# Turning 30 blocks by VectorE and transfers in place of TensorE transposes, in a two-layer decoder trunk

## The chip, the cores and the metric

The kernel runs on one core of a Trainium2 chip, as one program. The metric is the time of one execution in microseconds of the device. A core has TensorE (matrix products, and transposes as products with an identity), VectorE, ScalarE, GpSimd and SyncE, each with an instruction queue of its own that it works off in order, and 16 DMA engines for transfers. Transfers are issued here by SyncE (all weights), by GpSimd (rows and scratch) and a few by ScalarE.

## The reference

Two layers over 256 tokens of width 2048 and 256 memory tokens, in float32:

```python
h = x
for layer in range(2):
    u = rmsnorm(h, norm_mix[layer])
    mix = hgrn2_gdn_mixer(u, ...) if layer == 0 else mamba2_mixer(u, ...)
    h = h + mix
    h = h + memory_cross_attention(rmsnorm(h, norm_xattn[layer]), rmsnorm(mem, norm_mem[layer]),
                                   xa_wq[layer], xa_wk[layer], xa_wv[layer], xa_wo[layer])
    h = h + swiglu(rmsnorm(h, norm_ffn[layer]), ffn_w_gate[layer], ffn_w_up[layer], ffn_w_down[layer])
return rmsnorm(h, norm_final)

def swiglu(h, w_gate, w_up, w_down):              # 2048 -> 5632 -> 2048
    return (silu(h @ w_gate) * (h @ w_up)) @ w_down

def memory_cross_attention(h, m, wq, wk, wv, wo): # 4 heads of 128
    q, k, v = h @ wq, m @ wk, m @ wv
    p = softmax(q k^T / sqrt(128))                # per head
    return (p v) @ wo

def mamba2_mixer(u, ...):                         # 4096 inner, 8 groups of 512
    z, xbc, dt = split(u @ w_in)
    x, B, C = split(silu(conv(xbc) + bias))
    y = ssd_chunked(x, softplus(dt + dt_bias), -exp(a_log), B, C) + d_skip * x
    return rmsnorm(y * silu(z), norm_w) @ w_out
```

## The kernel before, in words

**Products.** TensorE does nearly everything. A float32 weight tile (128 x 1024 numbers, 512 KB, tile `wr`, four buffers) is loaded by SyncE's queue. `split` makes two tiles of a faster matmul type of it: `wh`, a cast by ScalarE (line 156), and `wl = wr - wh`, by VectorE (recorded at line 124); both have four buffers. Activations are kept as such a pair too, hi and lo, in `u` tiles (16 buffers of 4 x 256 numbers per partition). `xstat` (matmuls recorded at line 121) computes 256 tokens by 512 columns in two accumulators `acc`: for each 128 rows of the weights and each half of the tokens three matmuls, xh wh, xh wl and xl wh. A product over all 2048 rows is 16 x 2 x 3 = 96 matmuls, and one weight tile feeds 12.

**Turning.** `xstat` yields rows (tokens on partitions), but its own operand must have channels on partitions. So results are turned between products. `turned` (line 289) does it for one block, 2 x 128 tokens by 512 channels, with 8 `pe.transpose` of 128 x 128 into PSUM, in two calls of 4. Four kinds of block are turned:

- *Feed-forward activations.* `ffn` takes the 5632 hidden channels in 11 blocks, in groups of 4, 4 and 3. For each block: the gate product, SiLU by ScalarE into `sg` (tile `gate`, `raw` or `w`, in turn), the up product, and `sg = sg * up` by VectorE. `turn(sg)` is called one block later, between the gate and the up product of the next block, and for the last block of a group after its up product: `turned`, then `split` into a `u` pair (ScalarE copy, VectorE subtraction). Then the group is multiplied by its part of the down weights, added to `h` for four column blocks `nb`.
- *Residual blocks.* `RowNorm.block` turns a block of `h`, scales by the norm's gain (ScalarE writes hi, VectorE lo) and sums squares; it is called as each column block `nb` of a sub-layer's last projection is added to `h`. N3 feeds the second mixer, N4 the second cross-attention.
- *Gate blocks of the second mixer.* `ssd` works in 8 groups of 512 channels. `group` projects x, convolves it, builds decay matrices, computes y, and multiplies it by silu(z), where z comes through `columns`: `rows` evicts the product into the tile `raw` by ScalarE (line 403), `turned` turns `raw` into the PSUM tile `tn`, and VectorE multiplies. After four groups the first half of the output projection runs, after the other four the second half.
- *Queries and keys* of the two cross-attentions, through `columns` as well, copied by ScalarE into `cv` and `X`.

**Order.** The kernel is written in dataflow; a planner orders each engine's instructions by priority (program order) along a simulated timeline and inserts the waits. Engines then work in exactly that order. Tiles of one tag share its buffers, and a new tile waits until all readers of the one before are done.

Of the kernel before, what the change touches and what calls it, by code (L numbers as in the profile page):

```python
# [9 lines left out]
F32 = mybir.dt.float32  # L10
# [3 lines left out]
AF = mybir.ActivationFunctionType  # L14
ALU = mybir.AluOpType
# [3 lines left out]
P = 128  # L19
# [59 lines left out]
def trunk(ctx: ExitStack, tc: tile.TileContext, A: dict, out: bass.AP):  # L79
    nc = tc.nc  # L80
# [4 lines left out]
    up = ctx.enter_context(tc.tile_pool(name="u", bufs=16))  # L85
# [30 lines left out]
    def col(name, i=0, n=1):  # L116
        o = COLS[name][0] + i
        return cols[:, o:o + n]
# [4 lines left out]
    def tt(e, o, a, b, op):  # L123
        e.tensor_tensor(o, a, b, op=op)  # L124

    def stt(o, a, s, b, op0, op1):
        dve.scalar_tensor_tensor(o, a, s, b, op0=op0, op1=op1)  # L127

    def t4(tag, shape, dt=F32):
        return mp.tile(shape, dt, name=tag, tag=tag, bufs=BUFS.get(tag, 1))  # L130
# [24 lines left out]
    def split(hi, lo, src):  # L155
        act.copy(hi, src)  # L156
        tt(dve, lo, src, hi.bitcast(F32), ALU.subtract)
# [96 lines left out]
    class Norm:  # L254
# [9 lines left out]
        def block(self, nb):  # L264
            src = self.load(nb)
            hi, lo = utiles()
            for c in range(4):
                g = col(self.gain[0], self.gain[1] + nb * 4 + c)
                act.activation(hi[:, c], src[:, c], AF.Copy, scale=g)
                stt(lo[:, c], src[:, c], g, hi[:, c].bitcast(F32), ALU.mult, ALU.subtract)  # L270
            self.u.append((hi, lo))
# [10 lines left out]
    def turned(src, i, ps=None, late=0):  # L282

        if ps is None:
            ps = psb([P, 2, T])
        for x in range(2):
            c = 2 * i + x
            for a in range(2):
                ins = pe.transpose(ps[:, x, a * P:(a + 1) * P], src[a][:, c * P:(c + 1) * P], ident)  # L289
                if late:  # L290
                    later_in_stream(ins, late)
        return ps

    class RowNorm:


# [4 lines left out]
            self.ss = cp.tile([P, 2, 4], F32, name="rss", tag="rss", bufs=2)  # L301
            self.r = None

        def block(self, nb, src, late=0):
            op = utiles()
            hi, lo = op
            for i in range(2):
                ps = turned((src[:, 0], src[:, 1]), i, None, late)
                for x in range(2):
                    c = 2 * i + x  # L310
                    g = col(self.gain[0], self.gain[1] + nb * 4 + c)
                    act.activation(hi[:, c], ps[:, x], AF.Copy, scale=g)  # L312
                    stt(lo[:, c], ps[:, x], g, hi[:, c].bitcast(F32), ALU.mult, ALU.subtract)
            self.u.append(op)
            self.squares(nb, src)
# [91 lines left out]
    def rows(N, W, n0, func=AF.Copy, first=None):  # L407

        accs = xstat(W, n0, 512, N.u)
        if first:  # L410
            first()
        r = N.column()
        o = t4("raw", [P, 2, 512])
        o = [o[:, 0], o[:, 1]]
        evict(o, accs, r, func)
        return o

    def columns(N, W, n0, func=AF.Copy, first=None, late=0):

        o = rows(N, W, n0, func, first)  # L420
        for i in range(2):
            yield i, turned(o, i, pt.tile([P, 2, T], F32, name="tn", tag="tn"), late)

    def heads_by_token(N, W, n0, c0):

# [387 lines left out]
    def memory_keys(layer):  # L813

        def load_mem(nb):
            raw = wp.tile([P, 4, T], F32, name="wr", tag="wr", bufs=4)
            nc.sync.dma_start(raw, blk(A["memT"], nb))
            return raw

        M = Norm(("norm_mem", 16 * layer), load_mem, mem_r[0])  # L820
        k = t4("X", [P, 4, T])
        for i, ps in columns(M, ("xa_wk", layer), 0):
            act.copy(k[:, 2 * i:2 * i + 2], ps)
        return M, k

    def xattn(layer, N, nxt, keys=None):
        q = t4("cv", [P, 4, T])
        for i, ps in columns(N, ("xa_wq", layer), 0):
            act.copy(q[:, 2 * i:2 * i + 2], ps)
        M, k = keys or memory_keys(layer)  # L830
        pT = [t4(tg, [P, 4, T]) for tg in ("D", "MD")]
        pr = t4("kq", [P, 2, 4, T])
        sc = float(P) ** -0.5
        sm = cp.tile([P, 2, 4], F32, name="xsm", tag="xsm")
        mx = cp.tile([P, 2, 4], F32, name="xmx", tag="xmx")
        for a in range(2):
            for i in range(2):
                ps = psb([P, 2, T])
                for x in range(2):
                    m = 2 * i + x  # L840
                    mm(ps[:, x], q[:, m, a * P:(a + 1) * P], k[:, m])
                mi = mx[:, a, 2 * i:2 * i + 2]
                dve.tensor_reduce(mi, ps, axis=AX.X, op=ALU.max)
                dve.tensor_scalar(mi, mi, -sc, None, op0=ALU.mult)
                for x in range(2):
                    m = 2 * i + x
                    act.activation(pr[:, a, m], ps[:, x], AF.Exp, bias=mx[:, a, m:m + 1], scale=sc,
                                   accum_out=sm[:, a, m:m + 1])
        for a in range(2):
            dve.reciprocal(sm[:, a], sm[:, a])  # L850
            tt(dve, pr[:, a], pr[:, a], sm[:, a].unsqueeze(2).to_broadcast([P, 4, T]), ALU.mult)
            for b in range(2):
                ps = psb([P, 4, P])
                for m in range(4):
                    pe.transpose(ps[:, m], pr[:, a, m, b * P:(b + 1) * P], ident)
                (act.copy if b else dve.tensor_copy)(pT[b][:, :, a * P:(a + 1) * P], ps)
        v = gate_rows(M, ("xa_wv", layer), 0, AF.Copy, "XT")
        hi, lo = utiles()
        for i in range(2):
            ps = psb([P, 2, T])  # L860
            for x in range(2):
                m = 2 * i + x
                for b in range(2):
                    mm(ps[:, x], v[:, b, m * P:(m + 1) * P], pT[b][:, m], x == 0 and b == 0, b == 1)
            split(hi[:, 2 * i:2 * i + 2], lo[:, 2 * i:2 * i + 2], ps)
        project(("xa_wo", layer), [(hi, lo)], ((0, 4),), lambda nb: nxt.block(nb, h[nb]))


    def ffn(layer, N, done=None, parts=None, by_token=None):
        b0 = 0  # L870
        for nblk in (4, 4, 3):
            hid = []
            late = None

            def turn(sg):
                hi, lo = op = utiles()
                for i in range(2):
                    split(hi[:, 2 * i:2 * i + 2], lo[:, 2 * i:2 * i + 2], turned(sg, i))
                hid.append(op)

            for b in range(b0, b0 + nblk):
                ga = xstat(("ffn_w_gate", layer), 512 * b, 512, N.u)
                r = N.column()
                sg = t4(("gate", "raw", "w")[b % 3], [P, 2, 512])
                sg = (sg[:, 0], sg[:, 1])
                for a in range(2):
                    act.activation(sg[a], ga[a], AF.Silu, scale=r[:, a:a + 1])
                if late:
                    turn(late)
                ua = xstat(("ffn_w_up", layer), 512 * b, 512, N.u)  # L890
                for a in range(2):
                    stt(sg[a], ua[a], r[:, a:a + 1], sg[a], ALU.mult, ALU.mult)
                late = sg
            turn(late)
            last = b0 + nblk == 11
            project(("ffn_w_down", layer), hid, ((4 * b0, 4 * nblk),), done if last else None, parts if last else None)
            if last and by_token:
                project_by_token(("ffn_w_down", layer), hid, 4 * b0, 4 * nblk, parts, by_token)
            b0 += nblk


    def ssd(N, nxt):
# [30 lines left out]
        def group(g, bct):  # L933
# [22 lines left out]
            for half in range(2):  # L956
# [11 lines left out]
                for x in range(2):  # L968
                    m = 2 * half + x
                    stt(y[:, m], xc[:, m], col("ssd_d", 4 * g + m), ps[:, x], ALU.mult, ALU.add)  # L970
            for i, z in columns(N, W, 512 * g, AF.Silu):
                tt(dve, y[:, 2 * i:2 * i + 2], y[:, 2 * i:2 * i + 2], z, ALU.mult)
            hi, lo = utiles()
            for m in range(4):
                w = col("ssd_norm", 4 * g + m)
# [21 lines left out]
        for nb in range(4):  # L997
            accs = xstat(Wo, nb * 512, 512, ys, (KT, KT))
            for a in range(2):
                p, hb = part[nb][:, a], h[nb][:, a]  # L1000
                tt(dve, p, p, accs[a], ALU.add)
                stt(hb, p, r[:, a:a + 1], hb, ALU.mult, ALU.add)
            nxt.block(nb, h[nb])


    def load_x(nb):
# [24 lines left out]
    N2 = RowNorm(("norm_ffn", 0))  # L1031
    xattn(0, N1, N2, keys)
    N3 = RowNorm(("norm_mix", 16))
    ffn(0, N2, lambda nb: N3.block(nb, h[nb]))
    N4 = RowNorm(("norm_xattn", 16))
    ssd(N3, N4)
    N5 = RowNorm(("norm_ffn", 16))
# [83 lines left out]
```

## Time and profile before

| | |
|---|---|
| median of 3 runs | 2910.77 us (2910.56 to 2910.94) |
| profiled execution: time, span | 2911.57 us, 2909.8 us |
| TensorE busy, granted clock | 2891.2 us (99%), 0.998 |
| VectorE, ScalarE, GpSimd busy | 1770.2, 1457.6, 28.9 us |
| matmuls of `xstat` (line 121) | 7808 with wh and 3904 with wl |
| transposes of `turned` (line 289) | 608 |
| transferred | 542.36 MB, mean 186 GB/s |
| transfers issued by GpSimd | 14.69 MB, 1.6% of the 16 engines' span |

Engines: PE is TensorE's matmuls, PEld its weight loads, DVE VectorE, ACT ScalarE, POOL GpSimd, SP SyncE, and a q behind a name is the engine's queue. In a group "out<-in" names the tile written and the tiles read (`cst` holds the identity), then come partitions x elements, the count, busy us, mean ns of one, and the idle time before. Matmul records overlap, since matmuls are pipelined: what one costs is read from the starts, not from its length.

### The profile page before, as it was taken

The numbers are of one execution on the slowest core, as the hardware profiler recorded it, in microseconds if no ns is written. First come the engines' busy times: TensorE is split into PE (matmuls) and PEld (weight loads), VectorE is DVE, ScalarE is ACT, GpSimd is POOL, SyncE is SP. The second block draws the span as 40 slices with busy tenths as digits, with TensorE's granted clock in tenths as the row PEclk, the third lists the DMA queues.
The fourth block names the chain that finished last, engine by engine and source line by source line (L and its number), as shares of the span: only waits on it lengthen the run. The fifth ranks groups of instructions, "written<-read, shape, count | busy, mean of one in ns | idle before, by whom it ended". The sixth has DMA issues, their size and how long they took to land.

```text
span 2909.8 us, 35776 instructions
## 1 busy us (share of the span) xinstructions
PE 2891.2 (99%) x13656; PEld 2402.2 (83%) x13656; DVE 1770.2 (61%) x2287; ACT 1457.6 (50%) x1834; POOL 28.9 (1%) x61
## 2 busy tenths in 40 slices
PE   8999999999999999999999999999999999999998
PEld 7888888888888888888888888888888888888887
DVE  6676768865555445445677846787664454455455
ACT  7455547655443443444655645565564443443444
POOL 0000000000000000000000000000000000000000
PEclk9999999999999999999999999999999999999999
DMA  8554544545555555555655555545555555555554
GB/s 284 173 175 141 182 145 164 191 159 188 188 188 195 188 189 192 192 189 187 206 180 195 188 198 186 188 167 182 204 185 190 189 189 194 191 190 191 195 188 153
DMA packets 154749, 542.36 MB, mean 186 GB/s; under 512 B 16968, under 2 KB 23248, under 8 KB 154576
## 3 DMA queue, kind: packets, MB, share of 16 engines
q1 hardware_dynamic: 149872, 525.11, 52.2%
q0 software_dynamic: 4288, 14.69, 1.6%
q8 instruction: 107, 1.75, 0.2%
q14 instruction: 66, 0.54, 0.1%
q10 hardware_dynamic: 416, 0.27, 0.0%
HBM read 536.13 MB, written 3.87 MB: 186 GB/s over the span
## 4 chain that ended last, share of the span: by engine, by line
PE 98%; DVE 1%; ACT 1%; issue 0%; DMA 0%; SPq 0%; DVEq 0%
PE acc L121 91%; PE mx L121 4%; PE mx L289 1%; PE tn L289 1%; PE mx L952 0%; DMA wr<-in_hy_w_in 0%; DVE wl L124 0%; ACT wh L156 0%; DVE tmp L124 0%; PE mx L489 0%; DVE b L127 0%; PE mx L601 0%; DVE X L127 0%; DVE D L124 0%; ACT D L448 0%
## 5 line engine op out<-in xcount | busy, mean ns | idle before, releaser
L121 PE MATMUL acc<-wh,u 128*128 128x512 f32 x7808 | 2445.8, 393 | 7.2 <-ACT wh L156 7.2
L124 DVE TENSOR_TENSOR wl<-wr,wh 128x1024 fp32r<-128x1024 f32 x974 | 1191.3, 1224 | 979.3 <-ACT wh L156 975.9
L121 PEld LDWEIGHTS acc<-wh,u 128*128 128x128 f32 x7808 | 1465.0, 188 | 306.3 <-ACT wh L156 7.2
L156 ACT CAST wh<-wr 128x1024 fp32r<-128x1024 f32 x978 | 1025.6, 1050 | 1210.6 <-PE acc L121 1145.1
L121 PE MATMUL acc<-wl,u 128*128 128x512 f32 x3904 | 1530.8, 392 | 1.3 <-DVE wl L124 1.3
L121 PEld LDWEIGHTS acc<-wl,u 128*128 128x128 f32 x3904 | 735.2, 188 | 151.7 <-DVE wl L124 2.7
L127 DVE SCALAR_TENSOR_TENSOR cv<-tn,cols,cv 128x255 f32<-128x255 f32 (+2 forms) x120 | 57.6, 480 | 19.3 <-ACT cv L395 17.3
L124 DVE TENSOR_TENSOR h<-h,acc 128x512 f32<-128x512 f32 (+1 forms) x89 | 57.6, 675 | 10.5 <-PE acc L121 10.3
L403 ACT ACTIVATE raw<-acc,r 128x512 f32<-128x512 f32 x64 | 42.2, 684 | 23.7 <-PE tn L289 12.0
L127 DVE SCALAR_TENSOR_TENSOR u<-mx,cols,u 128x256 fp32r<-128x256 f32 x96 | 43.2, 479 | 10.4 <-ACT u L312 6.8
L312 ACT ACTIVATE u<-mx,cols 128x256 fp32r<-128x256 f32 x80 | 34.8, 469 | 20.5 <-PE mx L289 18.1
L289 PE MATMUL tn<-cst,raw 128*128 128x128 f32 x272 | 43.7, 272 | 1.0 <-ACT raw L403 1.0
L289 PEld LDWEIGHTS tn<-cst,raw 128*128 128x128 f32 x272 | 34.1, 139 | 10.2 <-ACT raw L403 1.4
L124 DVE TENSOR_TENSOR u<-mx,u 128x512 fp32r<-128x512 f32 x48 | 31.0, 684 | 12.2 <-ACT u L156 12.2
L156 ACT CAST u<-mx 128x512 fp32r<-128x512 f32 x48 | 26.0, 591 | 16.1 <-PE mx L289 10.7
L319 ACT ACTIVATE b<-h 128x512 f32<-128x512 f32 x48 | 29.9, 624 | 1.4 <-DVE h L127 1.4
L121 PEld LDWEIGHTS mx<-tmp 128*127 128x127 f32 (+7 forms) x240 | 24.8, 178 | 1.3 <-issue 0.7
L289 PE MATMUL mx<-cst,h 128*128 128x128 f32 x160 | 25.3, 272 | 0.0
L121 PE MATMUL mx<-tmp 128*127 128x64 f32 (+7 forms) x240 | 25.0, 260 | 0.0
L127 DVE SCALAR_TENSOR_TENSOR kq<-tn,cols,kq 128x255 f32<-128x255 f32 (+2 forms) x48 | 22.8, 475 | 2.4 <-ACT kq L395 2.0
L289 PEld LDWEIGHTS mx<-cst,h 128*128 128x128 f32 x160 | 20.0, 140 | 4.9
L395 ACT ACTIVATE cv<-tn,cols 128x256 f32<-128x256 f32 x40 | 18.6, 466 | 5.2 <-PE tn L289 3.9
(281 smaller groups left out, 1129.0 us busy)
## 6 DMA issues: line engine op xcount, KB each, us to landing
wr<-in_ffn_w_gate SPq DMA_DIRECT2D x176, 512.0 KB, 3.2
wr<-in_ffn_w_up SPq DMA_DIRECT2D x176, 512.0 KB, 3.2
wr<-in_ffn_w_down SPq DMA_DIRECT2D x176, 512.0 KB, 3.2
wr<-in_ssd_w_in SPq DMA_DIRECT2D x161, 512.0 KB, 3.3
wr<-in_hy_w_in SPq DMA_DIRECT2D x129, 512.0 KB, 3.3
wr<-in_ssd_w_out SPq DMA_DIRECT2D x64, 512.0 KB, 3.3
wr<-in_hy_w_out SPq DMA_DIRECT2D x32, 512.0 KB, 4.1
tmp<-rows POOLq DMA_DIRECT2D x18, 512.0 KB, 4.1
```

The costliest lines, as they stand in the source:

```text
L121: return pe.matmul(o, lhsT=lhsT, rhs=rhs, start=start, stop=stop, skip_group_check=True)
L124: e.tensor_tensor(o, a, b, op=op)
L127: dve.scalar_tensor_tensor(o, a, s, b, op0=op0, op1=op1)
L156: act.copy(hi, src)
L289: ins = pe.transpose(ps[:, x, a * P:(a + 1) * P], src[a][:, c * P:(c + 1) * P], ident)
L312: act.activation(hi[:, c], ps[:, x], AF.Copy, scale=g)
L319: act.activation(t4("b2", [P, 512]), src[:, a], AF.Square, accum_out=self.ss[:, a, nb:nb + 1])
L395: act.activation(c, x, AF.Copy, scale=w[:, 3:4])
L403: act.activation(o[a], accs[a], func, scale=r[:, a:a + 1])
```

## The change

A helper `turned_by_dma` turns a block without TensorE. VectorE transposes 32 x 32 blocks of both halves into y, four GpSimd-issued transfers write the four partition groups of y to a DRAM tile (1 KB runs), a fifth reads it back as z (4 KB per partition), and z has channels on partitions, in tokens by 32. y and z take the tiles named in `tags`, or two `u` buffers. `by32` is a view that matches the order. It is used for these blocks; all others stay on TensorE:

- feed-forward, both layers: every block but the last of each group, so 8 of 11 a layer;
- residual blocks: `nb` 0 to 2 of N3 and of N4, where the subtraction is also cut into halves of 128 tokens;
- gate blocks: three of each four groups, 6 of 8;
- the keys of layer 0 and the queries of layer 1.

```diff
+    def turned_by_dma(src, tags):
+        if tags:
+            y, z = t4(tags[0], [P, 1024]), t4(tags[1], [P, 1024])
+        else:
+            y, z = (up.tile([P, 1024], F32, name="ut", tag="u") for _ in range(2))
+        y, z = y.rearrange("p (b k a c) -> p b k a c", b=4, k=4, a=2), z.rearrange("p (q k c) -> p q k c", q=4, k=8)
+        for a in range(2):
+            dve.transpose(y[:, :, :, a, :].rearrange("p b k c -> p k b c"), src[a])
+        d = dp.tile([4, 32, 4, 256], F32, name="turns", tag="turns", bufs=2)
+        for q in range(4):
+            nc.gpsimd.dma_start(d[:, :, q].rearrange("b r x -> r b x"),
+                                y[32 * q:32 * q + 32].rearrange("r b k a c -> r b (k a c)"))
+        nc.gpsimd.dma_start(z.rearrange("p q k c -> p (q k c)"), d.rearrange("b r q x -> (b r) (q x)"))
+        return z.rearrange("p q k c -> p k q c")
+
+    AWAY = (("X", "cv"), ("tmp", "tmp"))
+
+    def by32(x):
+        return x.rearrange("p k (a q c) -> p (k a) q c", a=2, q=4)
...
-        def block(self, nb, src, late=0):
+        def block(self, nb, src, late=0, tags=None):
             op = utiles()
             hi, lo = op
-            for i in range(2):
+            if tags:
+                z = turned_by_dma((src[:, 0], src[:, 1]), tags)
+                for c in range(4):
+                    g, x = col(self.gain[0], self.gain[1] + nb * 4 + c), z[:, 2 * c:2 * c + 2]
+                    act.activation(by32(hi[:, c:c + 1]), x, AF.Copy, scale=g)
+                    for a in range(2):
+                        stt(by32(lo[:, c:c + 1])[:, a], x[:, a], g, by32(hi[:, c:c + 1])[:, a].bitcast(F32), ALU.mult, ALU.subtract)
+            for i in range(0 if tags else 2):
                 ps = turned((src[:, 0], src[:, 1]), i, None, late)
...
+    def columns_by_dma(N, W, n0, func=AF.Copy, tags=None):
+        z = turned_by_dma(rows(N, W, n0, func), tags)
+        for i in range(2):
+            yield i, z[:, 4 * i:4 * i + 4]
...
-        for i, ps in columns(M, ("xa_wk", layer), 0):
-            act.copy(k[:, 2 * i:2 * i + 2], ps)
+        if layer:
+            for i, ps in columns(M, ("xa_wk", layer), 0):
+                act.copy(k[:, 2 * i:2 * i + 2], ps)
+        else:
+            for i, z in columns_by_dma(M, ("xa_wk", layer), 0, tags=("tmp", "w")):
+                act.copy(by32(k[:, 2 * i:2 * i + 2]), z)
...
-            def turn(sg):
+            def turn(sg, b):
                 hi, lo = op = utiles()
-                for i in range(2):
-                    split(hi[:, 2 * i:2 * i + 2], lo[:, 2 * i:2 * i + 2], turned(sg, i))
+                if b < b0 + nblk - 1:
+                    z = turned_by_dma(sg, AWAY[b % 2])
+                    for i in range(2):
+                        split(*(by32(x[:, 2 * i:2 * i + 2]) for x in op), z[:, 4 * i:4 * i + 4])
+                else:
+                    for i in range(2):
+                        split(hi[:, 2 * i:2 * i + 2], lo[:, 2 * i:2 * i + 2], turned(sg, i))
                 hid.append(op)
...
-            for i, z in columns(N, W, 512 * g, AF.Silu):
-                tt(dve, y[:, 2 * i:2 * i + 2], y[:, 2 * i:2 * i + 2], z, ALU.mult)
+            away = g % 4 < 3
+            for i, z in (columns_by_dma if away else columns)(N, W, 512 * g, AF.Silu):
+                o = by32(y[:, 2 * i:2 * i + 2]) if away else y[:, 2 * i:2 * i + 2]
+                tt(dve, o, o, z, ALU.mult)
...
-            nxt.block(nb, h[nb])
+            nxt.block(nb, h[nb], 0, AWAY[nb % 2] if nb < 3 else None)
...
-    ffn(0, N2, lambda nb: N3.block(nb, h[nb]))
+    ffn(0, N2, lambda nb: N3.block(nb, h[nb], 0, AWAY[nb % 2] if nb < 3 else None))
```

The queries of `xattn` are changed like the keys, with the layers the other way round.

More of the change, by code (lines that the diff above doesn't have):

```diff
@@ L827, in xattn @@
         q = t4("cv", [P, 4, T])
-        for i, ps in columns(N, ("xa_wq", layer), 0):
-            act.copy(q[:, 2 * i:2 * i + 2], ps)
+        if layer:
+            for i, z in columns_by_dma(N, ("xa_wq", layer), 0, tags=("tmp", "w")):
+                act.copy(by32(q[:, 2 * i:2 * i + 2]), z)
+        else:
+            for i, ps in columns(N, ("xa_wq", layer), 0):
+                act.copy(q[:, 2 * i:2 * i + 2], ps)
         M, k = keys or memory_keys(layer)
@@ L873, in ffn @@
             late = None
-            def turn(sg):
+            def turn(sg, b):
                 hi, lo = op = utiles()
-                for i in range(2):
-                    split(hi[:, 2 * i:2 * i + 2], lo[:, 2 * i:2 * i + 2], turned(sg, i))
+                if b < b0 + nblk - 1:
+                    z = turned_by_dma(sg, AWAY[b % 2])
+                    for i in range(2):
+                        split(*(by32(x[:, 2 * i:2 * i + 2]) for x in op), z[:, 4 * i:4 * i + 4])
+                else:
+                    for i in range(2):
+                        split(hi[:, 2 * i:2 * i + 2], lo[:, 2 * i:2 * i + 2], turned(sg, i))
                 hid.append(op)
@@ L888, in ffn @@
                 if late:
-                    turn(late)
+                    turn(late, b - 1)
                 ua = xstat(("ffn_w_up", layer), 512 * b, 512, N.u)
@@ L893, in ffn @@
                 late = sg
-            turn(late)
+            turn(late, b)
             last = b0 + nblk == 11
```

## The prediction

> **What bounds the kernel now.** I read the page's first part, its chain, and then the waits of TensorE and of ScalarE. The first two lines below are the page's head and its first part, the third heads its chain. The others are waits: who waited for whom, total us, times, longest us.
>
> ```profile
> span 2909.8 us, 35776 instructions
> ...
> PE 2891.2 (99%) x13656; PEld 2402.2 (83%) x13656; DVE 1770.2 (61%) x2287; ACT 1457.6 (50%) x1834; POOL 28.9 (1%) x61
> ...
> PE 98%; DVE 1%; ACT 1%; issue 0%; DMA 0%; SPq 0%; DVEq 0%
> ```
> ```profile
> ACT wh L156 <- PE acc L121: 1145.1, 702, 5.0
> ...
> PE acc L121 <- ACT wh L156: 7.2, 1, 7.2
> PE acc L121 <- DVE wl L124: 1.3, 2, 0.9
> PE tn L289 <- ACT raw L403: 1.0, 1, 1.0
> ```
> TensorE is never out of work: 18.6 us of the span are not busy, and its longest wait, 7.2 us, happened once. The weight casts of ScalarE wait for TensorE instead, 702 times: each stands ready until a weight buffer comes free. So a matmul taken off TensorE shortens the kernel by the time it takes there, provided nobody else becomes late, and work added to VectorE, ScalarE, GpSimd or the transfers costs nothing until it makes TensorE wait.
>
> **What is removed.** One block (512 channels of 256 tokens) is turned by 8 transposes of 128x128. The lines view has them all, by target and source (busy us, mean ns); the chain in order of time shows what a block costs.
>
> ```profile
> L289 PE MATMUL tn<-cst,raw 128*128 128x128 f32 x272 | 43.7, 272 | 1.0 <-ACT raw L403 1.0
> ...
> L289 PE MATMUL mx<-cst,h 128*128 128x128 f32 x160 | 25.3, 272 | 0.0
> ...
> L289 PE MATMUL mx<-cst,raw 128*128 128x128 f32 x64 | 8.9, 272 | 0.0
> ...
> L289 PE MATMUL mx<-cst,gate 128*128 128x128 f32 x64 | 8.6, 272 | 0.0
> ...
> L289 PE MATMUL mx<-cst,w 128*128 128x128 f32 x48 | 6.2, 273 | 0.0
> ```
> ```profile
> 728.68 43.58 PE acc L121 x192
> 773.13 43.54 PE acc L121 x192
> ```
> ```profile
> 1346.50 0.22 PE mx L289 x2
> 1346.72 0.23 PE acc L121
> 1346.95 0.66 PE mx L289 x6
> ```
> ```profile
> 1566.53 0.44 PE tn L289 x4
> ```
> In the feed-forward blocks the first run of matmuls ends at 728.68 + 43.58 = 772.26 and the next begins at 773.13, so 8 transposes take 0.87 us. A residual block takes 0.22 + 0.66 = 0.88 us, and a block that goes through tile tn 2 x 0.44 = 0.88 us. That is 0.11 us each, though each record is 272 ns long: the records overlap.
>
> The count: a feed-forward layer has groups of 4, 4 and 3 blocks and keeps the last of each on TensorE, so 3 + 3 + 2 = 8 go per layer, 16 in two (128 of the 64 + 64 + 48 = 176 transposes). Three residual blocks go before the second mixer and three behind it (48 of 160); six gate blocks, one of keys and one of queries go from tile tn (64 of 272). Together 30 blocks, 240 transposes, 30 x 0.88 = 26.4 us, all on the path that sets the end.
>
> [...]
>
> **What takes its place, per block.** Two VectorE transposes of 128x512 (32x32 within themselves), four GpSimd-issued writes of 128 KB to DRAM, then, behind all four, one read of 512 KB, and then the same copies and subtractions as before, from SBUF rather than PSUM. The nearest rows, from the lines view and from the DMA part (KB, us from issue to landing):
>
> ```profile
> L658 DVE STREAM_TRANSPOSE XT<-X 128x512 f32<-128x512 f32 x4 | 2.8, 707 | 0.1
> ...
> L661 DVE STREAM_TRANSPOSE XT<-X 32x128 f32<-32x128 f32 x8 | 2.4, 303 | 0.2
> ```
> ```profile
> L635 POOL DMA_DIRECT2D X<-scratch x4 | 3.0, 761 | 5.4 <-PE acc L121 3.6 <-DMA scratch<-b 1.9
> ```
> ```profile
> q1 hardware_dynamic: 149872, 525.11, 52.2%
> ...
> scratch<-MD POOLq DMA_DIRECT2D x4, 256.0 KB, 3.1
> X<-scratch POOLq DMA_DIRECT2D x4, 256.0 KB, 5.6
> ```
> ```profile
> L127 DVE SCALAR_TENSOR_TENSOR u<-mx,cols,u 128x256 fp32r<-128x256 f32 x96 | 43.2, 479 | 10.4 <-ACT u L312 6.8
> ...
> L127 DVE SCALAR_TENSOR_TENSOR b<-mx,hms,gate 128x128 f32<-128x128 f32 x24 | 6.5, 344 | 0.1
> ```
> A transpose that writes in pieces costs between 0.71 us (the plain one) and 4 x 0.303 = 1.21 us (four of the small ones for 512 columns). I take 0.71, the same element count. VectorE gets 30 x 1.41 = 42 us, at most 73. In the six residual blocks 8 subtractions of 128 columns replace 4 of 256: 8 x 0.344 - 4 x 0.479 = 0.84 us each, 5 us together. ScalarE keeps its instructions. VectorE goes from 61% to about 62.5% of the span.
>
> GpSimd issues 150 more transfers, 150 x 0.76 = 114 us beside its 28.9: off the path. The read waits at the head of GpSimd's queue for the writes, and what is queued behind it are the next turn's writes and, in the mixer, the row loads of the next heads. The engines that carry the transfers are at 52% for the weight queue. The turns move 30 x 1 MB, 31.5 MB on 525 MB, so about 3 points more at the same rate. I put no price on that; against the weights it would have to hold up their loads, which are prefetched four deep.
>
> The length of one turn: 1.41 (transposes) + 4 x 0.76 (issues) + 3.1 (last write) + 5.6 (read) = 13.2 us; at most 14.2 with the slower transposes. Then come the consumers.
>
> **Where that is hidden.** For a turn to cost nothing, 13.2 us plus the consumers must fit between the source's last write and the first read of the result. Rows of the timeline (start us, us), in the order residual, gate, keys, queries:
>
> ```profile
> 1376.42 0.68 DVE L124 TENSOR_TENSOR h<-h,acc 128x512 f32<-128x512 f32 x1
> 1393.31 3.04 PE L121 MATMUL acc<-u,wh 128*128 128x256 f32 x24
> ```
> ```profile
> 1541.99 0.69 ACT L403 ACTIVATE raw<-acc,r 128x512 f32<-128x512 f32 x1
> 1561.64 0.68 DVE L124 TENSOR_TENSOR X<-X,tn 128x512 f32<-128x512 f32 x1
> ```
> ```profile
> 555.90 1.37 ACT L403 ACTIVATE raw<-acc,mem_r 128x512 f32<-128x512 f32 x2 [0.94 <-PE acc L121]
> 615.51 0.81 PE L121 MATMUL mx<-X,cv 128*128 128x256 f32 x3
> 2092.84 1.25 ACT L403 ACTIVATE raw<-acc,r 128x512 f32<-128x512 f32 x2
> 2125.73 1.03 PE L121 MATMUL mx<-X,cv 128*128 128x256 f32 x4
> ```
> Feed-forward: the turn of the last but one block of a group is handed over, at the latest, behind the last block's gate product. Its up product follows, half of the 192 matmuls above, 21.8 us, before the down projection starts, which reads that block as its second or third. 13.2 fits.
>
> Gates: 1542.7 to 1561.6 is 18.9 us, 5.7 to spare. Keys have 58 us, queries 31.
>
> Residual: the tight one is the third block before the second mixer. h is ready at 1377.1, and the small product at 1393.3 reads that block from its 17th matmul, about 1395.3: 18.2 us, for 13.2 plus about 2.5 of copies and subtractions (eight of 0.344 us). If VectorE is a weight subtraction late, or a landing slower, TensorE loses 0 to 3 us there, once. I take 1, as the margin of 2.5 is about as large as either. The other residual blocks have a whole block's matmuls more.
>
> **The sum.** 26.4 removed, 1 given back: 25.4. The profiled execution took 2911.57 us (span 2909.8 and 1.8 around it), 0.8 above the median of the runs. So 2886.2 for a profiled execution, 2885.4 against the median of 2910.77: forecast 2885.5. The bounds of this case alone: 0 to 5 us given back, and at most 2 us more gained where matmuls just behind transposes run slower; 2882 to 2890.
>
> **Rivals.**
> *A queue blocked by a late transfer (slower).* ScalarE and VectorE take instructions in a written order that an estimate of the transfers fixed. If a turn lands later than booked, the copy out of z stands at the head of ScalarE's queue (in the gates, the product on VectorE's), and the weight casts and subtractions behind it stop. The trace shows what such a stop costs:
>
> ```profile
> 322.53 1.23 DVE L124 TENSOR_TENSOR wl<-wr,wh 128x1024 fp32r<-128x1024 f32 x1 [1.50 <-ACT wh L156]
> 329.42 0.71 DVE L638 STREAM_TRANSPOSE XT<-X 128x512 f32<-128x512 f32 x1 [5.66 <-DMA X<-scratch]
> 330.05 1.18 DVE L124 TENSOR_TENSOR wl<-wr,wh 128x1024 fp32r<-128x1024 f32 x1
> ```
> VectorE stood 5.66 us for a transfer, its weight subtraction came 6.3 us after the previous one had ended, and TensorE has no wait there. So a cushion of about 6 us is proven. The rival needs a stop above 6 + 25.4/30 = 6.9 us on average in all 30 turns, half the turn's 13.2. With 8 us it is 30 x 2 = 60 lost, 34.6 net, 2945 us. For it: a turn has two transfers in a row, and neither their shape nor their booking is in this trace. Against it: the same round through DRAM cost 0.34 to 5.66 us of waiting here, the latter behind an issue that was itself 3.6 us late.
>
> *VectorE becomes the bound in the mixer.*
> ```profile
> 1550.00:1600.00 50.00, 50.00 (x254) 40.93 (x253) 39.96 (x54) 30.08 (x40) 1.06 (x2) 1.00 0.57 189
> ```
> In a steady stretch of groups (columns PE, PEld, DVE, ACT) VectorE is busy 39.96 of 50 us; 1.41 more is 41.4. It has room, but it works in bursts. If each of the six turned gates cost TensorE the transposes' time and its two wl waits' worth, 6 x (1.4 + 1.3) = 16 us, the end is 2902.
>
> *The turns never cost anything on the path* (transposes only filled time in which TensorE would otherwise wait for the same data): no change, 2910. Against it: the matmuls follow the transposes without a wait in all three stretches of the chain.
>
> [...]
>
> **How the numbers follow.** Everything covered, 2882 to 2890: 0.70. Part of it lost, VectorE's bursts or a few late turns, 2890 to 2904: 0.13. No change: 0.06. Blocked queues, slower: 0.09. The transposes cost their full records, 2846: 0.02. A measurement tells about 0.2%, 5.8 us, from no change. So faster 0.84, same 0.07, slower 0.09. The range runs from 2880 to 2902: the likeliest case with a little more gain below, most of the second above, which leaves out just under 2 in 10.
>
> **What the next profile must show.** 368 instead of 608 matmuls on L289; the chain still 98% TensorE; matmul runs joining without the 0.88 us gaps; span about 2884. VectorE near 1817 us busy, GpSimd near 140. TensorE's waits under 15 us; if they grow to tens of us with a release by the weight cast or subtraction, and the copies out of z wait for a DMA above 6 us, the first rival is right. Stops of VectorE between 1450 and 2020 without DMA waits mean the second. Wrong also if landings of 128 KB writes are far above 3.1 us.

## The result and the profile after

The changed kernel took 2888.43 us (median; 2883.85 to 2896.71) against 2910.77: a ratio of 0.9929, with a 95% interval of 0.9918 to 0.994. That is 22.3 us less, 2.9 above the forecast of 2885.5 and inside the range of 2880 to 2902. The profiled execution took 2889.2 us. In some executions TensorE's granted clock drops near 255 us (0.79 from 250 to 260 in the profile of before, 1.00 in that of after), which costs 3.2 us in work that neither kernel changes (last section); the profiled execution of before has this drop, that of after has not.

The page's head, its first part, the queues and the chain of the changed kernel:

```profile
span 2887.2 us, 35683 instructions
...
PE 2864.5 (99%) x13416; PEld 2372.5 (82%) x13416; DVE 1798.7 (62%) x2371; ACT 1456.2 (50%) x1834; POOL 112.5 (4%) x211
...
q1 hardware_dynamic: 149872, 525.11, 56.5%
...
PE 93%; DMA 3%; DVE 2%; ACT 1%; issue 1%; POOL 0%; DVEq 0%; SPq 0%; POOLq 0%; ACTq 0%
```

TensorE lost 240 matmul instructions (13656 to 13416) and 26.7 us of busy time, but the span fell by 22.6 only, and the chain now runs 93% over TensorE instead of 98%: some transfers have come into it. Which ones, the waits show (who waited for whom: us in total, times, longest us):

```profile
ACT wh L156 <- PE acc L121: 1014.2, 640, 5.5
...
ACT u L156 <- DMA cv<-turns: 48.0, 10, 6.4
...
ACT u L156 <- DMA tmp<-turns: 26.2, 6, 4.9
...
ACT u L334 <- DMA cv<-turns: 19.9, 4, 5.6
...
PE acc L121 <- ACT wh L156: 6.7, 1, 6.7
PE acc L121 <- DVE wl L124: 4.6, 5, 2.2
PE tn L289 <- ACT raw L433: 1.0, 1, 1.0
PE acc L121 <- ACT u L334: 0.8, 1, 0.8
```

ScalarE now stands for the read behind a turn in all 16 feed-forward blocks (line 156, 10 + 6 times) and in the residual blocks (line 334). TensorE's own waits grew by 4 us: five for VectorE's weight part instead of two, and one for a residual copy. That one and four of the five (at 1372, 1435, 2073 and 2094 us) lie behind the residual blocks.

Where the time came from and where it went shows in the chain in order of time (start us, us, what). The landmarks are the first product of the first feed-forward, the first of the second, and the 302 matmuls in one run behind the second; the first fence is of before.

```profile
668.59 59.22 PE acc L121 x261
...
2178.82 59.21 PE acc L121 x261
...
2840.59 60.81 PE acc L121 x302
```
```profile
663.13 172.78 PE acc L121 x762
...
1338.23 7.15 DMA cv<-turns
1353.99 6.60 DMA wr<-in_ffn_w_down
1361.80 4.89 DMA tmp<-turns
1374.91 6.62 DMA turns<-X
1382.10 5.45 DMA cv<-turns
1388.14 13.99 PE acc L121 x67
...
2163.44 172.77 PE acc L121 x762
...
2818.05 60.81 PE acc L121 x302
```

The second feed-forward takes 654.6 us instead of 661.8: 7.2 less for 8 blocks, 0.90 each, and its runs of matmuls are no longer broken by transposes (762 in one go instead of 261). From the first feed-forward's start to the second's there are 21 blocks (8 feed-forward, 6 residual, 6 gate, 1 of queries). At 0.90 each that should give 18.9; it went from 1510.2 to 1500.3, 9.9. So 9 us were given back in there. (Ahead of the first feed-forward 5.5 us were gained, of which the turned block of keys explains 0.9 and the clock drop 3.2; the remaining 1.4 is there before anything changed runs. Of the 22.6 us between the two spans 18.0 are the change's.) The chain says where the 9 us went: between 1338 and 1388 it runs through three reads of turned residual blocks (`cv` and `tmp`), a write of one (`turns`) and one weight load.

Here is that stretch on ScalarE (timeline: start us, us, instruction; in brackets idle before and its releaser):

```profile
1345.40 1.71 ACT L334 ACTIVATE u<-cv,cols 128x256 fp32r<-128x256 f32 x4 [4.48 <-DMA cv<-turns]
...
1360.69 1.06 ACT L156 CAST wh<-wr 128x1024 fp32r<-128x1024 f32 x1 [3.45 <-DMA wr<-in_ffn_w_down]
1366.71 1.71 ACT L334 ACTIVATE u<-tmp,cols 128x256 fp32r<-128x256 f32 x4 [4.96 <-DMA tmp<-turns]
...
1387.58 1.71 ACT L334 ACTIVATE u<-cv,cols 128x256 fp32r<-128x256 f32 x4 [4.45 <-DMA cv<-turns]
```
and VectorE and TensorE behind the second stop, with the stage's windows (us; busy us and count of PE, PEld, DVE, ACT, POOL; granted clock; DMA share; GB/s):
```profile
1367.25 0.61 DVE L127 SCALAR_TENSOR_TENSOR u<-tmp,cols,u 128x128 fp32r<-128x128 f32 x2 [4.25 <-ACT u L334]
...
1371.18 1.18 DVE L124 TENSOR_TENSOR wl<-wr,wh 128x1024 fp32r<-128x1024 f32 x1
```
```profile
1372.42 0.74 PE L121 MATMUL acc<-wl,u 128*128 128x512 f32 x1 [2.21 <-DVE wl L124]
1372.95 0.63 PE L121 MATMUL acc<-wh,u 128*128 128x512 f32 x1
1373.38 0.63 PE L121 MATMUL acc<-wl,u 128*128 128x512 f32 x1
```
```profile
1370.00:1375.00 5.00, 2.79 (x7) 2.10 (x7) 5.00 (x8) 2.99 (x5) 1.72 (x4) 0.75 0.29 93
1375.00:1380.00 5.00, 5.00 (x21) 4.02 (x20) 1.52 (x3) 1.27 (x2) 0.46 (x1) 0.91 0.91 279
```

This is the prediction's first rival at work. The copy out of z stands at the head of ScalarE's queue for 4.48 us. The weight casts behind it catch up, but one of them meets a late weight load (3.45 us more), and 6 us later the next block's copy stops ScalarE again, 4.96 us. VectorE's subtractions wait behind that, then do their residual work first, and the weight subtraction at 1371.18 is too late: TensorE stands 2.21 us. It pays a second time: the matmuls behind the wait start 0.43 us apart (1372.95, 1373.38) instead of 0.23, at a granted clock of 0.75 and 0.91 over those windows (0.50 over the 3.4 us from 1372.5 on). Take from a window's length the time that its matmuls need at full rate (0.227 us each for 512 columns, as in the 762 in 172.78 us above); call what is left the excess. The stretch from 1200 to 1440 has an excess of 6.9 us after and 0.7 before; the one around the second set (1985 to 2215; in before 1995 to 2230) has 5.0 after and 2.0 before. The differences, 6.2 and 3.0, make 9.2 us, the 9 that are missing.

### The profile page after: what moved, and what is told of

Read it like the earlier page. It is cut to its first block, busy times and chain, and to the rows that moved or that the text cites. A ratio compares the mean times of both kernels' runs of the same rounds, so it can differ in the third digit from the quotient of the medians.

```text
span 2887.2 us, 35683 instructions
## 1 busy us (share of the span) xinstructions
PE 2864.5 (99%) x13416; PEld 2372.5 (82%) x13416; DVE 1798.7 (62%) x2371; ACT 1456.2 (50%) x1834; POOL 112.5 (4%) x211
## 4 chain that ended last, share of the span: by engine, by line
PE 93%; DMA 3%; DVE 2%; ACT 1%; issue 1%; POOL 0%; DVEq 0%; SPq 0%; POOLq 0%; ACTq 0%
PE acc L121 87%; PE mx L121 4%; PE tn L289 1%; DVE wl L124 1%; DMA cv<-turns 1%; DMA wr<-in_memT 1%; DMA turns<-X 1%; PE mx L289 1%; DVE u L127 0%; ACT wh L156 0%; DMA tmp<-turns 0%; PE mx L1001 0%; DMA wr<-in_ffn_w_down 0%; POOL turns L306 0%; DMA tmp<-rows 0%
## 5 line engine op out<-in xcount | busy, mean ns | idle before, releaser
L306 POOL DMA_DIRECT2D turns<-X x56 | 30.6, 553 | 1226.7 <-DVE X L303 1223.0
L124 DVE TENSOR_TENSOR u<-cv,u 128x512 fp32r<-128x512 f32 x20 | 12.9, 688 | 42.0 <-ACT u L156 42.0
L127 DVE SCALAR_TENSOR_TENSOR u<-mx,cols,u 128x256 fp32r<-128x256 f32 x72 | 32.6, 477 | 6.4 <-ACT u L534 3.5
L156 ACT CAST u<-cv 128x512 fp32r<-128x512 f32 x20 | 11.4, 619 | 48.0 <-DMA cv<-turns 48.0
L306 POOL DMA_DIRECT2D turns<-tmp x40 | 21.9, 554 | 332.4 <-DVE tmp L303 332.4
L289 PE MATMUL tn<-cst,raw 128*128 128x128 f32 x208 | 33.8, 272 | 1.0 <-ACT raw L433 1.0
L289 PEld LDWEIGHTS tn<-cst,raw 128*128 128x128 f32 x208 | 26.2, 140 | 8.3 <-ACT raw L433 1.4
L342 ACT ACTIVATE u<-mx,cols 128x256 fp32r<-128x256 f32 x56 | 24.7, 466 | 11.9 <-PE mx L289 11.8
L306 POOL DMA_DIRECT2D turns<-ut x24 | 13.3, 561 | 317.3 <-DVE ut L303 317.3
```

What stands on the lines that cost most here:

```text
L306: nc.gpsimd.dma_start(d[:, :, q].rearrange("b r x -> r b x"), y[32 * q:32 * q + 32].rearrange("r b k a c -> r b (k a c)"))
```

## The experiments

**Parts of the change alone.** Beside the next four kernels the kernel before took 2910.57 us.

Feed-forward alone (16 blocks; the first two edits are the keys and the queries):
```diff
-        if layer:
+        if True:
...
-        if layer:
+        if False:
...
-            away = g % 4 < 3
+            away = False
...
-            nxt.block(nb, h[nb], 0, AWAY[nb % 2] if nb < 3 else None)
+            nxt.block(nb, h[nb])
...
-    ffn(0, N2, lambda nb: N3.block(nb, h[nb], 0, AWAY[nb % 2] if nb < 3 else None))
+    ffn(0, N2, lambda nb: N3.block(nb, h[nb]))
```


> Only the 16 feed-forward blocks are turned by VectorE and transfers. Theory A (a turned block frees 0.88 us everywhere; what was lost was lost around the residual blocks alone): 14.1 us off, 2896.7. Rival B (every turn blocks the queues a little, 20.7 us over 30 blocks is 0.69 a block): 11.0 off, 2899.8. Both may be 3.2 us lower if TensorE's clock does not drop near 255 us, where it dropped in the profile of before.

Measured: 2896.04 us, ratio 0.9951 (0.9938 to 0.9963), 14.5 less: 0.91 per block. TensorE has the waits of before and no other. ScalarE's stops for the read, 16 of them and up to 5.3 us long, are all there and cost nothing.

Residual blocks alone (6 blocks):
```diff
-                if b < b0 + nblk - 1:
+                if False:
```
with the first three edits of the one above (keys, queries, gates), and without its last two.

> Only the six residual blocks are turned by VectorE and transfers. Theory A: 5.3 us freed, about 8 us lost to a dry TensorE and its lower clock behind it, 2913 to 2914, not faster than before. Rival B: 6 x 0.69 us off, 2906.7.

Measured: 2910.0 us, ratio 0.9997 (0.9988 to 1.0006), from 2901.75 to 2912.15 but for one execution of 5039.42. Six blocks off TensorE gain nothing: about 5 us are lost, not the 8 expected. Timeline of ScalarE and of TensorE in that kernel, and its windows:
```profile
1358.36 1.71 ACT L334 ACTIVATE u<-cv,cols 128x256 fp32r<-128x256 f32 x4 [5.70 <-DMA cv<-turns]
...
1381.25 1.70 ACT L334 ACTIVATE u<-tmp,cols 128x256 fp32r<-128x256 f32 x4 [7.46 <-DMA tmp<-turns]
```
```profile
1383.94 1.22 PE L121 MATMUL acc<-wh,u 128*128 128x512 f32 x2 [2.29 <-ACT wh L156]
1386.96 0.80 PE L121 MATMUL acc<-wl,u 128*128 128x512 f32 x1 [1.80 <-DVE wl L124]
```
```profile
1380.00:1385.00 5.00, 2.71 (x10) 1.53 (x8) 3.21 (x10) 3.75 (x9) 0.00 (x0) 0.87 0.01 4
1385.00:1390.00 5.00, 3.20 (x8) 2.48 (x8) 5.00 (x7) 2.53 (x5) 2.18 (x4) 0.50 0.39 125
```
Two stops 23 us apart, 5.70 and 7.46 us; behind the second TensorE waits 2.29 and 1.80 us and runs five microseconds at a clock of 0.50. What six blocks bring, about 5.5 us, is spent there. Behind the second mixer the stops of this execution were shorter (3.38, 3.06 and 4.38 us, 12 and 23 us apart), and TensorE has no added wait there: the length of the stops counts as well as their distance. The DMA share of 0.01 is no scarcity of the engines: with the casts stopped no weight buffer comes free, so no load is issued (in the profile of after SyncE's loads wait for VectorE's weight part 17 times between 1330 and 1400, up to 9.0 us).

Everything but the residual blocks (24 blocks):
```diff
-            nxt.block(nb, h[nb], 0, AWAY[nb % 2] if nb < 3 else None)
+            nxt.block(nb, h[nb])
...
-    ffn(0, N2, lambda nb: N3.block(nb, h[nb], 0, AWAY[nb % 2] if nb < 3 else None))
+    ffn(0, N2, lambda nb: N3.block(nb, h[nb]))
```

> All of the change but the residual blocks, which stay on TensorE. Theory A: 5.3 us more of transposes and 8 us less of stalls, 2885 to 2886, and the runs lie closer together. Rival B: 24 x 0.69 us off, 2894.2, slower than the whole change.

Measured: 2884.9 us, ratio 0.9919 (0.9906 to 0.9933). With six blocks fewer turned away it is no slower than the full change (2888.43; 2890.2 where it ran again, below). TensorE's waits are those of before, the longest:
```profile
PE acc L121 <- ACT wh L156: 7.0, 1, 7.0
```

Gates alone (6 blocks): the residual edits just shown, keys and queries as in the first kernel, and
```diff
-                if b < b0 + nblk - 1:
+                if False:
```

> Only the six gate blocks are turned by VectorE and transfers. Theory A: 5.3 us off, 2905.5. Rival B: 2906.7. The prediction's second rival (VectorE's bursts in the mixer cost TensorE time): no gain, 2911 or more.

Measured: 2904.73 us, ratio 0.9979 (0.997 to 0.9988), 5.8 less, 0.97 per block; TensorE waits once for the weight cast, 6.5 us, as in before. The second rival, VectorE's bursts, would have had this one slower than before (16 us lost on 5.3 removed). In the full change a steady stretch shows the room that is left (1550 to 1600, columns as above; VectorE, third, 40.51 of 50 us):
```profile
1550.00:1600.00 50.00, 50.00 (x249) 40.84 (x248) 40.51 (x56) 31.38 (x40) 4.35 (x7) 1.00 0.66 211
```

**Transfers or the wait for them.** The six residual blocks are turned both ways: VectorE transposes, 24 writes and 6 reads stay, but the operand comes from TensorE's transposes as before, and nobody reads z. All other blocks stay on TensorE, by the edits of the kernel with residual blocks alone.
```diff
             if tags:
                 z = turned_by_dma((src[:, 0], src[:, 1]), tags)
-                for c in range(4):
...
-            for i in range(0 if tags else 2):
+            for i in range(2):
```


> All blocks are turned by TensorE as before; the six residual blocks are turned by VectorE and transfers as well, and that second result is read by nobody. Theory A (what costs is the copy that stands at the head of ScalarE's queue until the transfers land): no wait, the time of before, 2910.6, within 1 us, TensorE's waits as before. Rival C (the added transfers slow the weight loads, or VectorE's added transposes are too much there): as slow as with the six blocks in use and their 5.5 us not gained, 2914 to 2916.

Measured: 2910.39 us beside 2910.42 for the kernel before, ratio 0.9998 (0.9989 to 1.0007), waits as in before. Nothing is removed from TensorE here, so no gain was to be had; the point is that nothing is lost either. The transposes on VectorE, GpSimd's issues and the transfers of these blocks are free. What is left of the second kernel is ScalarE and VectorE standing for the read, and VectorE's eight small subtractions in place of four; the next kernel keeps those subtractions and takes the standing away.

**Take the wait away.** The copies of a residual block are ordered behind the squares of the next block on ScalarE, so the read has a whole column block of time to land before its turn in the queue comes. The third block before the second mixer, which has no such slack, goes back to TensorE (29 blocks).
```diff
+                self.pending = nb, turned_by_dma((src[:, 0], src[:, 1]), tags)
...
+            last = self.squares(nb, src)
+            if before:
+                n, z = before
...
-                    act.activation(by32(hi[:, c:c + 1]), x, AF.Copy, scale=g)
+                    ins = act.activation(by32(hi[:, c:c + 1]), x, AF.Copy, scale=g)
+                    behind(ins, last)
...
-    ffn(0, N2, lambda nb: N3.block(nb, h[nb], 0, AWAY[nb % 2] if nb < 3 else None))
+    ffn(0, N2, lambda nb: N3.block(nb, h[nb], 0, AWAY[nb % 2] if nb < 2 else None))
```


> The change, but in the residual blocks the copies out of z are ordered behind the next block's sums of squares on ScalarE, about a block later, and the third block before the second mixer stays on TensorE: 29 blocks. Theory A: nothing waits at the head of the queue for the residual blocks, 5 x 0.92 us better than the kernel without them (2884.9): 2880.3. Rival C: like the change or the kernel without residual blocks, 2885 to 2888.

Measured: 2881.1 us, ratio 0.9905 (0.9891 to 0.9918), the shortest median of all, but of four executions only. The profiled one has the clock drop near 255 us and took 2886.01, the other three about 2881. Profile against profile, with 3.2 us taken off for the drop, it is 2.5 us shorter than the kernel without residual blocks (2888.48, also with the drop) and 3.1 shorter than the change run again (2885.89, without it; next kernel). Before the second mixer the copies find their data, and ScalarE has no idle time ahead of them; behind it the first copy still waits:
```profile
1350.92 1.69 ACT L350 ACTIVATE u<-cv,cols 128x256 fp32r<-128x256 f32 x4
1371.31 1.70 ACT L350 ACTIVATE u<-tmp,cols 128x256 fp32r<-128x256 f32 x4
...
2020.38 1.71 ACT L350 ACTIVATE u<-cv,cols 128x256 fp32r<-128x256 f32 x4 [7.57 <-DMA cv<-turns]
```
The excess of the stretch 1200 to 1440 falls from 6.9 to 0.8 us, as without residual blocks (0.6). In the second set the first two column blocks end 6 us apart, so "behind the next block's squares" is no delay there; the stop of 7.57 us costs TensorE two short waits, 0.52 and 0.76 us, and the stretch keeps 3.7 of excess.

The change itself, again on the same chip: 

> The change itself, on the chip of the other kernels of this call: 2888.4, runs spread over some 10 us. A second clock drop near 255 us or none moves a run by about 4 us.

Measured: 2890.2 us, ratio 0.9927 (0.9915 to 0.994). The three stops before the second mixer are shorter, 1.81, 3.67 and 4.78 us instead of 4.48, 4.96 and 4.45, and the excess there 3.9 instead of 6.9. The second stop costs TensorE nothing in this execution; the loss starts with the third block, where TensorE waits for the copy itself:
```profile
PE acc L121 <- ACT u L334: 1.1, 1, 1.1
```
The loss hangs on when a read lands, and varies from one execution to the next.

**One stop or a series.** Only the first residual block of each set is turned away (26 blocks):
```diff
-            nxt.block(nb, h[nb], 0, AWAY[nb % 2] if nb < 3 else None)
+            nxt.block(nb, h[nb], 0, AWAY[nb % 2] if nb < 1 else None)
...
-    ffn(0, N2, lambda nb: N3.block(nb, h[nb], 0, AWAY[nb % 2] if nb < 3 else None))
+    ffn(0, N2, lambda nb: N3.block(nb, h[nb], 0, AWAY[nb % 2] if nb < 1 else None))
```

> The change with only the first residual block of each set by VectorE and transfers, 26 blocks. Theory A: a single stop fits the cushion, the loss needs a second one before the weight buffers are full again: 2 x 0.92 us better than without residual blocks (2884.9), 2883.1. Rival D (one stop is enough): 2884.9 to 2888.

Measured: 2885.51 us, ratio 0.9916 (0.9901 to 0.9932), from 2883.59 to 2887.07 but for one execution of 7510.88. The median is 2.4 above what was expected and lies in the rival's range, so the times alone do not decide; the traces do. TensorE has no added wait behind these blocks, and the excess of both stretches is 0.8 and 1.9, as without residual blocks. The profiled execution, 2883.59 without the clock drop, is 1.7 us shorter than that of the kernel without residual blocks once the drop's 3.2 us are taken off 2888.48; 1.8 was expected. The two stops were 1.97 and 4.92 us here: a single stop of that length fitted the prefetch, and two in a row in the change, 4.48 and 4.96 us, drained it.

**One step further.** The later copies with the third block on TensorE in the second set as well (28 blocks), so on top of the edits of the later copies:
```diff
-            nxt.block(nb, h[nb], 0, AWAY[nb % 2] if nb < 3 else None)
+            nxt.block(nb, h[nb], 0, AWAY[nb % 2] if nb < 2 else None)
```

> As e6_later_copies, and the third block before the second cross-attention is on TensorE too: 28 blocks, two residual ones a set. In e6_later_copies ScalarE stood 7.6 us for that third block and TensorE lost about 1.7 us of work time around it. Theory A: that loss goes, 0.9 us of transposes come back, 0.8 better than e6_later_copies: about 2880.3 without the clock drop near 255 us, 2884.3 with it; TensorE's waits as before. Rival D (the loss there is not that block's copy): 0.9 slower than e6_later_copies, 2882, with the waits unchanged.

Measured: 2887.39 us, ratio 0.9923 (0.9909 to 0.9936): above both expectations. Its profile (2888.39) is 2.4 us longer than that of the later copies; both have the clock drop. The first copy of the second set still stops, 7.10 us, so the third block was not what cost there. One block more on TensorE explains 0.9 of it; the rest was lost in the second feed-forward. Timelines of GpSimd and ScalarE:
```profile
2551.41 0.56 POOL L306 DMA_DIRECT2D turns<-X  x1 [35.56 <-DVE X L303]
2554.45 1.64 POOL L306 DMA_DIRECT2D turns<-X  x3 [2.49 <-issue]
```
```profile
2567.77 1.14 ACT L156 CAST u<-cv 128x512 fp32r<-128x512 f32 x2 [7.98 <-DMA cv<-turns]
```
GpSimd paused 2.49 us between a turn's first write and the other three, for nothing that the profile shows. The read came that much later, the stop grew to 7.98 us, and TensorE, waiting 0.34 us for a cast and 0.76 for a weight subtraction, lost about 1.6 us over that stretch. What caused the pause stays open. It is not new: the change, its second run, the later copies and the first residual blocks alone each have one such pause of 2.49 us in the second feed-forward, at another block, and the stops behind it are their longest there, 6.44, 6.95, 6.64 and 6.87 us. So these stops show where the cushion ends. Up to 6.64 us TensorE did not wait; behind 6.87 and 6.95 us it waited 0.27 and 0.34 us; the stops of 7.10, 7.57 and 7.98 us cost 1 to 2 us each.

## Why the prediction came out as it did

The number came out inside the prediction's likeliest branch, 2882 to 2890 with everything covered, but not for that branch's reason: part of the gain was lost, as in the branch that was given 0.13 and 2890 to 2904. A block brought a little more than forecast, the loss reached or passed its upper bound of 5, and the two errors partly cancel. That is in part luck.

*The price of a block* was slightly under-read. 0.88 us was the gap in the chain; the runs show 0.90 (second feed-forward), 0.91 (feed-forward alone), 0.97 (gates alone). The bounds had up to 2 us for slower matmuls just behind transposes (in the profile of before the first one behind eight took 0.32 us to the next start, 728.43 to 728.75, instead of 0.23); at 0.91 for 30 blocks it is 27.3 instead of 26.4. No run shows transposes that cost the whole length of their records, the branch of 2846 us: eight of them brought 0.90 to 0.97 us, with records of 272 ns each.

*The given-back term was mis-sized.* The prediction put 1 us, with 0 to 5, at one place: the third residual block before the second mixer. It measured about 9 us between the profiles of before and after, about 5.5 in the second profile of the change, and about 5 in the medians (27.3 less 22.3), where it is not known which executions had the clock drop. The place was right in part: the third block did make TensorE wait for its copy, 0.8 us, and 1.1 in the second profile, where no other wait came ahead of it. In the first profile the larger part came from the blocks ahead of it and behind the second mixer, which the text called safe because their readers on TensorE come much later. That step looked only at who reads the result. The copy out of z stands in ScalarE's queue in its written place, and everything behind it waits, whoever needs it.

*The first rival* named just this and was given 0.09, for all 30 turns. It acts, but in six. Its threshold was good: the cushion was put at 6 us, and single stops were free up to 6.64 us and cost first 0.3 us of waiting at 6.9. The stops of the change came to 1.4 to 6.4 us, so the 16 in the feed-forward pass. The residual blocks break it below the threshold, since the second stop comes 20 us after the first, before the weight buffers have filled again: between the two a cast waited 3.45 us for its load, and in the kernel with residual blocks alone two waited 2.10 and 2.19 us. A threshold for one stop was used for a series of them; the traces with one and with three blocks per set tell these apart.

*The length of a turn* was 13.2 us, at most 14.2. The GpSimd rows and the landings (KB, us) give another split:
```profile
1353.15 2.19 POOL L306 DMA_DIRECT2D turns<-tmp  x4 [14.37 <-DVE tmp L303]
1361.80 0.56 POOL L308 DMA_DIRECT2D tmp<-turns  x1 [6.46 <-ACT wh L156]
```
```profile
turns<-X POOLq DMA_DIRECT2D x56, 128.0 KB, 4.8
cv<-turns POOLq DMA_DIRECT2D x14, 512.0 KB, 5.3
```
An issue took 0.55 us, less than the 0.76 taken, and the read 5.3 against 5.6. The write of 128 KB took 4.8, by tile between 3.9 and 4.8 in the median (3.1 taken, from a row of 256 KB writes), and 6.46 us passed between the last write's issue and the read's. (The row names a weight cast as the releaser; in the trace the last of the four writes lands at 1361.22, 0.58 us ahead of the read.) From the transposes at 1350.4 to the copy at 1366.7 it is 16.3 us. The gates' 18.9 and the keys' and queries' covers held even so.

*VectorE, GpSimd, transposes.* VectorE came to 1798.7 us busy, not 1817, though each transpose took 0.70 as put; neighbours' records overlap, so busy time grew by 28.5 us while the sum of the records grew by 43. GpSimd has 112.5 instead of 140 (the cheaper issue). L289 has 208 + 112 + 32 + 16 = 368 matmuls, as counted.
TensorE's waits, put at under 15 us, sum to 14.4 in the view. The chain at 93% instead of 98% was the sign that something else was in it.

*The transfers' bandwidth* got no price, rightly as far as the six residual blocks go: turned twice and read by nobody, they cost nothing. The loads of weights did become slower, 3.2 to 4.2 us for the feed-forward gate's:
```profile
wr<-in_ffn_w_gate SPq DMA_DIRECT2D x176, 512.0 KB, 4.2
```
Four buffers at 2.7 us each (an estimate from 12 matmuls of 0.227 us) hide that, until a stop has emptied them: then one such load was the 3.45 us between the two stops.

## What to carry to other kernels

Work moved off the engine that bounds onto a long round of transfers was gained in full here only where every instruction that consumes the result stood late enough in its own engine's queue (0.91 us a block in the feed-forward alone, 0.6 us in all from the six residual blocks alone): ask what is queued behind the consumer, not only who needs its output. The prefetch was a cushion for one stop, of up to 6.64 us here, so compare a stop with the cushion and the distance between stops with the time to refill it; here stops of 4 to 6 us some 44 us apart were free, and stops of about 5 us some 20 us apart were not in every execution. Where the slack exists but the queue hides it, write the consumer behind the next block's work (about 3 us shorter than the change, profile against profile), and leave on the fast engine the blocks that have none.

## What the runs showed of the hardware

A short wait cost TensorE more than its length here. Behind 2.21 us of idle time 512-column matmuls started 0.43 us apart instead of 0.23 for 3.4 us, with a granted clock of 0.50; nearly as much was lost to the slow clock (eight matmuls in 3.5 us instead of 1.8) as to the wait. In the kernel with residual blocks alone two waits of 2.29 and 1.80 us went with 6.8 us at 0.50 (a mean of 0.69 from 1380 to 1390 and of 0.97 from 1390 to 1400). Behind waits of 0.76 us (the change) and 1.1 us (its second run) the clock stayed at 1.00. No run shows from what length of wait on the clock drops, or what sets how long it stays down.

The clock also drops early in some executions. TensorE does 32 matmuls of one column each there, 4.1 us in the profile of before, in which it counts as busy but does little. While they run the clock drops in that profile, to 0.50 for 6.8 us from 255.7 on; in the profile of after it does not (the instruction and the windows of before, then the window of after; columns as above):
```profile
252.77 4.14 PE L121 MATMUL mx<-ones,tmp 128*128 128x1 f32 x32
```
```profile
250.00:260.00 10.00, 10.00 (x57) 8.83 (x57) 5.51 (x16) 8.23 (x12) 0.00 (x0) 0.79 0.48 159
260.00:270.00 10.00, 10.00 (x43) 7.90 (x42) 7.10 (x18) 2.85 (x3) 0.00 (x0) 0.87 0.18 56
```
```profile
250.00:260.00 10.00, 10.00 (x68) 8.96 (x68) 6.50 (x23) 7.71 (x11) 0.00 (x0) 1.00 0.45 155
```
From the first of these matmuls to the next transposes of `cv` it is 10.9 us in the profile of before (252.77 to 263.67) and 7.7 in that of after (251.19 to 258.87): the drop cost 3.2 us there, in work that neither kernel changes. Of the eleven profiles seven have it (0.69 to 0.79 from 250 to 260) and four have not (1.00), with the same matmuls in all; that these matmuls bring it about is not shown, and what decides is not shown either.
